# A one-core hybrid attention and state-space block: denser attention pieces, inputs loaded three ahead, and six split tiles

## The chip, the cores and the metric

The kernel runs on one core of one Trainium2 chip. The metric is device time in microseconds (us), the median of several runs; a profiled execution gives the trace.

## The reference

One layer of a residual block on 256 tokens of width 4096. All products are in float32 accuracy.

```python
h = rms_norm(x, pre_norm_gain)
proj = h @ w_in                                   # one projection, columns split into:
(q, k, v, gate_a, qi, ki, wi, z, xs, bm, cm, dt_raw, merge_logits) = split(proj)
q, k, qi, ki = (apply_rope(a) for a in (q, k, qi, ki))
attn = dsa_attention(q, k, v, qi, ki, wi * scale) # indexer: top 64 keys of each query, then softmax
y_a  = attn * silu(gate_a)
y_b  = ssd_mixer(xs, z, bm, cm, dt_raw, ...)      # Mamba-2 scan, gated and normed
gates = sigmoid(merge_logits)                     # one gate of width 4096 for each branch
merged = gates[0] * (y_a @ w_branch_attn) + gates[1] * (y_b @ w_branch_ssd)
x + rms_norm(merged @ w_out, post_norm_gain)
```

## The kernel before

**The matmuls.** Each float32 matrix is held as a high and a low part, and a product is three matmuls (low x high, high x low, high x high) of 128x512 on the matrix engine (PE). The inputs are split once; the weights are split as they stream in: a `raw` tile of 512 KB is loaded on the SP queue, ACT rounds it into `wh`, DVE subtracts for `wl`. There are four `wh` and four `wl` buffers of two rows of weights each (`SBUFS`). `gemm` does 512 output columns in this way (`w_qi`, the first q and k columns, the last two of `w_out`).

**Pairs.** `pair_gemm` does 1024 output columns over 256 inner rows a step. A step of kind S is a Strassen-like form with 7 products (21 matmuls of PE) and needs an `ext` tile of input combinations; kinds D and R have 8 products (24 matmuls). An S step costs DVE more, since it also combines weights. The tuples `SX`, `SY`, `SM`, `SG` say which of the 16 steps are of kind S in which stage; those named `plain` are done as R there. A POOL-issued DMA adds one weight row to another for each S step.

**The order of the stages:** `w_qi` and the small columns with the indexer's scores and top-k; q and k of the first group; then for four groups of heads `w_qk[j]` and `w_vg[j]`; `w_z` and `w_x` with the state-space work; eight `w_gate` pairs; eight branch pairs (`w_br`, for two groups of output columns n the attention branch and then the SSD branch); three `w_out2` pairs and the two `w_out` columns.

**Pieces.** Everything that is not a weight matmul (rotation, attention, scan, the combination of inputs) is a Python generator of small pieces in the queue `aux`. A stage calls `step(pace)` once a step of kind S and twice a step of kind D or R; `pace` pieces are emitted at each call, with a carried fraction. The attention of group j (`attend`: 18 pieces, each a few instructions, and a last one that writes `yraw` to DRAM scratch `yscr`) is queued when `w_vg[j]` ends, so it runs in the next pair, `w_qk[j+1]` or, for the last group, `w_z[0]`. The list scheduler of the framework then settles each engine's order, which is fixed from there on.

**The end of a pair.** `early` is emitted behind the last S step: it drains what is left of the pieces, takes the four output tiles (`outs`) and starts to combine the PSUM banks into them, with one ACT copy and two DVE additions (lines 545 to 547). In `w_qk` and `w_z[0]` these output tiles are `yr0` to `yr3`; `attend` uses `yr0` for its result, `yr1` and `yr2` as `yraw`, and `yr3`.

**Inputs of the later stages.** `forms_from` turns 256 rows of branch input (from `yscr`, during the last `w_gate` pair and the first branch pair) or of merged input (from `mscr`, during the last branch pairs and `w_out2[0]`) into a split base tile and, for S steps, an `ext` tile. It loads one 256 KB tile `fr` ahead of the one that it works on, by a DMA on the POOL queue, into two buffers. `ev_branch` makes the merged input: sigmoid times product, summed over the two branches, transposed into `mT`, and written to `mscr` in one DMA for each 512 columns.

Of the kernel before, what the change touches and what calls it, by code (L numbers as in the profile page):

```python
# [17 lines left out]
P = 128  # L18
# [29 lines left out]
def fused_block(tc, x, xT, w_qi, w_misc, w_q0, w_qk, w_vg, w_x, w_z, w_gate, w_br, w_out2, w_out,  # L48
# [98 lines left out]
    def load_half(raw, chunk, hf, each=False):  # L147
# [3 lines left out]
        else:  # L151
            nc.sync.dma_start(raw, chunk[:, hf * HK:(hf + 1) * HK, :])

    def gemm(chunks, nk, act, evac, prep=None, plan=None, done=None, pace=1):
        while len(live) > 1:
            drain(live.popleft())
# [5 lines left out]
        for n, (half, toks) in enumerate(plan):  # L162
            c, hf = divmod(half, KC // HK)
            if half not in raws:
                raws[half] = raw_tile()
                if prep is not None:
                    if not hf:
                        xr = prep_x(c)
                    load_half(raws[half], chunks[c], hf, c == 0)
                else:  # L170
                    load_half(raws[half], chunks[c], hf)
            if half not in parts:
                wh = whp.tile([P, HK, NW], F32R, tag="wh", name="wh")
                wl = wlp.tile([P, HK, NW], F32R, tag="wl", name="wl")
                parts[half] = wh, wl
                if len(parts) > SBUFS:
                    del parts[next(iter(parts))]
                rs = raws[half]
                if prep is not None:
                    for i in range(HK):  # L180
                        split_x(half * HK + i, xr[:, hf * HK + i, :])
                        A.activation(wh[:, i, :], rs[:, i, :], AF.Copy)  # L182
                        V.tensor_sub(wl[:, i, :], rs[:, i, :], wh[:, i, :].bitcast(F32))
                else:
                    A.activation(wh, rs, AF.Copy)  # L185
# [57 lines left out]
    mb = [attp.tile([P, (t + 1) * P], F32, name=f"mb{t}") for t in range(2)]  # L243
    qip_cm, qip = open_pool("qip", bufs=2)
    startp, sp = open_pool("startp", bufs=2)

    def prep_x(c):
        xr = sp.tile([P, KC, S], F32, tag="xr", name="xr")
# [399 lines left out]
        turn(mode)  # L648

    def forms_from(what, load, seven, pairs, diff=True):  # L650
        a = load(pairs[0])
        for i in pairs:
            ahead = load(i + 1) if i + 1 in pairs else None
            make_base(i, a)
            yield
            make_ext(i, a, seven, diff)
            kind_of[i] = what
            a = ahead
            yield

    def kinds(seven, pairs, plain=()):
# [156 lines left out]
    for j in range(4):  # L818
        if j:
            pair_gemm("x", "aux", lambda i: w_qk[j - 1, i], kinds(SX, range(16)), yr4_after(0),  # L820
                      ev_qk(j))
        pair_gemm("x", "aux", lambda i: w_vg[j, i], kinds(SX, range(16)), yr4_after(4), ev_vg(j), pace=0.4)


# [175 lines left out]
    def z_pair(m, seven, outs, hooks={}, pace=1.25):  # L1000
# [2 lines left out]

    more = [i for i in SX if i not in SS]
    z_pair(0, SX, yr4_after(0), {more[-1] + 1: lambda: push(remake(
        more, SS, lambda: attp.tile([P, 2, S], F32, tag="lm", bufs=2, name="fr")))}, 1)
    drain()
    attp_cm.__exit__(None, None, None)
    ssdp_cm, ssdp = open_pool("ssdp")
# [15 lines left out]
        return run  # L1025

    def load_y(i):
        a = tp.tile([P, 2, S], F32, tag="fr", bufs=2, name="fr")
        nc.gpsimd.dma_start(a.rearrange("p k t -> p (k t)"), yscr[i])
        return a  # L1030

    def load_m(i):
        a = tp.tile([P, 2, S], F32, tag="fr", bufs=2, name="fr")
# [6 lines left out]
    def grow():  # L1040
        for n, i in enumerate(grown):
            ext_tag[i] = f"eg{n}"
        return remake(grown, SG, lambda: tp.tile([P, 2, S], F32, tag="fr", bufs=2, name="fr"))

    for g, cols in enumerate(GATES):
        last = g == len(GATES) - 1
# [44 lines left out]
    def ev_branch(n, br):  # L1091
        def run(c):
# [12 lines left out]
                for _ in range(4):  # L1105
                    yield
            for b in range(2):
                if (n, b) == (6, 1):
                    m2 = [brp.tile([P, 2, S], F32, tag=f"sg{h}", name="mT") for h in range(2)]
                    for t in range(2):  # L1110
                        transpose4(c[2 * t + b], m2[0][:, :, t * P:(t + 1) * P], A,
                                   m2[1][:, :, t * P:(t + 1) * P])
                        yield
                    merged.update({14 + h: m2[h] for h in range(2)})
                    continue
                mT = brp.tile([P, 4, S], F32, tag="mT", name="mT")
                for t in range(2):
                    transpose4(c[2 * t + b], mT[:, :, t * P:(t + 1) * P], A)
                    yield
                if n < 6:  # L1120
                    nc.scalar.dma_start(mscr[n + b], mT.rearrange("p k t -> p (k t)"))
                else:
                    for h in range(2):
                        merged[2 * (n + b) + h] = mT[:, 2 * h:2 * h + 2, :]
            yield
        return run

# [22 lines left out]

    def open_og():
        ogp["cm"], p = open_pool("ogp")
        ogp["og"] = [[p.tile([P, 2, NW], F32, name=f"og{t}_{n}") for n in range(3)]
                     for t in range(2)]
        ogp["oss"] = p.tile([P, 2, 8], F32, name="oss")
        V.memset(ogp["oss"], 0.0)

    def ogs(n):
        def run():
            og = ogp["og"]  # L1160
            return [og[t][n // 2][:, b, :] for t in range(2) for b in range(2)]
# [17 lines left out]

    for n in range(0, 6, 2):  # L1180
        if n == 0:
            order = (0, 2, 5, 1, 3, 8, 4, 9, 6, 11, 7, 10, 12, 13, 14, 15)
            plain = (9, 10, 14)
        else:
            order, plain = range(16), ()
        plan = [(i, "R" if k == "D" else k) for i, k in kinds(SM, order, plain)]
# [178 lines left out]
```

## Time and profile before

| | us |
|---|---|
| median of 3 runs (2848.03 to 2849.34) | 2849.27 |
| the profiled execution, its own time | 2850.78 |
| its span, first to last instruction | 2849.0 |
| PE busy | 2795.8 (98%) |
| DVE busy | 2514.9 (88%) |
| ACT busy | 1801.8 (63%) |
| mean granted TensorE clock | 0.994 |

A busy share is a mean over stages; the time of a stage is read against what its matmuls take in a stage that holds nothing else. The matmuls overlap on PE, so the length of one in a row is longer than the distance from one to the next.

### The profile page before, as it was taken

The page shows a single profiled execution, that of the slowest core. Times are in us where ns is not written, and L with a number is a line of the kernel's source. Part 1 is how long each engine was busy: PE and PEld are TensorE (multiplying, and loading weights), DVE is VectorE, ACT ScalarE, POOL GpSimd, SP SyncE. Part 2 cuts the span into 40 slices and gives each one's busy share as a digit, 9 for nine tenths or more (in the row PEclk, how much of TensorE's full clock was granted, in tenths as well). Part 3 has the DMA queues.
Part 4 walks back from the last instruction along what each step waited for, and adds up shares of the span by engine and source line. Part 5 has one row for each costly group of instructions (what it writes and reads, how often), then busy time and mean ns, then how long its engine had stood idle before and what let it go on. Part 6 is the DMA issues. An engine that isn't in the chain of part 4 may idle for free.

```text
span 2849.0 us, 36823 instructions
## 1 busy us (share of the span) xinstructions
PE 2795.8 (98%) x12597; PEld 2287.5 (80%) x12597; DVE 2514.9 (88%) x3326; ACT 1801.8 (63%) x2533; POOL 222.1 (8%) x265
## 2 busy tenths in 40 slices
PE   9999999999999999999999999999999999999998
PEld 7877787787877878787888788888877888878886
DVE  6668998998989979898898999999977999988975
ACT  7444565665656756878788866666655655655653
POOL 0100000000000000000000010110100000000000
PEclk9999999999999999999999999999999999999999
DMA  9545776776767767666767788888877888877874
GB/s 366 187 162 167 212 228 203 237 219 198 233 199 239 219 199 222 187 209 207 230 183 216 221 256 252 255 250 258 269 232 243 253 266 271 263 221 234 266 260 140
DMA packets 205756, 650.41 MB, mean 228 GB/s; under 512 B 23168, under 2 KB 23936, under 8 KB 205568
## 3 DMA queue, kind: packets, MB, share of 16 engines
q1 hardware_dynamic: 163728, 567.05, 59.3%
q0 software_dynamic: 34064, 65.29, 13.2%
q10 hardware_dynamic: 7776, 15.73, 1.4%
q8 instruction: 98, 1.61, 0.2%
q14 instruction: 90, 0.74, 0.1%
HBM read 628.06 MB, written 19.92 MB: 227 GB/s over the span
## 4 chain that ended last, share of the span: by engine, by line
PE 79%; DVE 10%; issue 6%; DMA 3%; ACT 2%; POOL 0%; SPq 0%; DVEq 0%; ACTq 0%; POOLq 0%
PE p L541 66%; PE p L194 3%; PE p L196 3%; PE p L195 3%; DVE wl L498 2%; DVE raw L610 1%; DMA yscr<-yraw 1%; DVE wl L186 1%; DMA fr<-yscr 1%; DVE raw L609 1%; ACT wh L494 1%; DVE wl L612 1%; DMA fr<-mscr 1%; DVE wl L605 1%; PE p L364 0%
## 5 line engine op out<-in xcount | busy, mean ns | idle before, releaser
L541 PE MATMUL p<-wh,b 128*128 128x512 f32 x4330 | 1428.7, 394 | 1.0 <-ACT wh L494 0.5
L494 ACT ACTIVATE wh<-raw 128x1024 fp32r<-128x1024 f32 (+1 forms) x1117 | 1052.8, 970 | 592.5 <-DVE raw L609 280.1
L498 DVE TENSOR_TENSOR wl<-raw,wh 128x1024 fp32r<-128x1024 f32 (+1 forms) x890 | 953.7, 1088 | 60.4 <-ACT wh L494 53.7
L541 PEld LDWEIGHTS p<-wh,b 128*128 128x128 f32 x4330 | 815.9, 188 | 173.8 <-ACT wh L494 5.0
L541 PE MATMUL p<-wl,b 128*128 128x512 f32 x2165 | 848.0, 392 | 10.3 <-DVE wl L496 8.0
L541 PE MATMUL p<-wh,ext 128*128 128x512 f32 x2396 | 806.9, 392 | 14.1 <-DVE pc L546 12.8
L541 PEld LDWEIGHTS p<-wh,ext 128*128 128x128 f32 x2396 | 451.2, 188 | 110.9 <-DVE pc L546 15.4
L541 PEld LDWEIGHTS p<-wl,b 128*128 128x128 f32 x2165 | 408.4, 189 | 96.4 <-DVE wl L496 10.4
L541 PE MATMUL p<-wl,ext 128*128 128x512 f32 x1198 | 473.8, 395 | 8.3 <-DVE wl L612 7.5
L496 DVE SCALAR_TENSOR_TENSOR wl<-raw,wh 128x1024 fp32r<-128x1024 f32 x227 | 276.9, 1220 | 39.2 <-ACT wh L494 38.1
L541 PEld LDWEIGHTS p<-wl,ext 128*128 128x128 f32 x1198 | 225.5, 188 | 68.2 <-DVE wl L612 16.3
L610 DVE TENSOR_TENSOR raw<-raw 128x1024 f32<-128x1024 f32 x221 | 270.3, 1223 | 5.6
L186 DVE TENSOR_TENSOR wl<-raw,wh 128x1024 fp32r<-128x1024 f32 x112 | 138.8, 1239 | 90.3 <-ACT wh L185 90.1
L604 ACT ACTIVATE wh<-raw 128x512 fp32r<-128x512 f32 x221 | 138.8, 628 | 105.4 <-PE p L541 97.7
L185 ACT ACTIVATE wh<-raw 128x1024 fp32r<-128x1024 f32 x112 | 118.3, 1058 | 136.3 <-PE p L196 124.5
L194 PE MATMUL p<-wh,b 128*128 128x512 f32 x512 | 202.1, 396 | 2.0 <-ACT wh L182 2.0
L195 PE MATMUL p<-wl,b 128*128 128x512 f32 x512 | 200.0, 391 | 0.0
L196 PE MATMUL p<-wh,b 128*128 128x512 f32 x512 | 199.8, 390 | 0.0
L605 DVE TENSOR_TENSOR wl<-raw,wh 128x512 fp32r<-128x512 f32 x221 | 151.5, 685 | 16.8 <-ACT wh L604 15.7
L609 DVE TENSOR_TENSOR raw<-raw 128x512 f32<-128x512 f32 x221 | 152.2, 689 | 5.0
L612 DVE TENSOR_TENSOR wl<-raw,wh 128x512 fp32r<-128x512 f32 x221 | 151.1, 684 | 0.0
L606 ACT ACTIVATE wh<-raw 128x512 fp32r<-128x512 f32 x221 | 136.3, 617 | 0.0
(243 smaller groups left out, 1841.4 us busy)
## 6 DMA issues: line engine op xcount, KB each, us to landing
raw<-w_gate_d SPq DMA_DIRECT2D x256, 512.0 KB, 5.7
raw<-w_vg_d SPq DMA_DIRECT2D x128, 512.0 KB, 5.5
raw<-w_x_d SPq DMA_DIRECT2D x128, 512.0 KB, 5.1
raw<-w_br_d SPq DMA_DIRECT2D x128, 512.0 KB, 5.5
raw<-w_out_d SPq DMA_DIRECT2D x128, 512.0 KB, 5.2
raw<-w_qk_d SPq DMA_DIRECT2D x96, 512.0 KB, 5.6
raw<-w_z_d SPq DMA_DIRECT2D x64, 512.0 KB, 5.5
raw<-w_qi_d SPq DMA_DIRECT2D x62, 512.0 KB, 5.2
```

The costliest lines, as they stand in the source:

```text
L186: V.tensor_sub(wl, rs, wh.bitcast(F32))
L194: T.matmul(ps[t], al[:, tk], wh[:, i, :], start=first, stop=False)
L195: T.matmul(ps[t], ah[:, tk], wl[:, i, :], start=False, stop=False)
L196: T.matmul(ps[t], ah[:, tk], wh[:, i, :], start=False, stop=last)
L494: A.activation(h, src, AF.Copy, scale=float(sign))
L496: V.scalar_tensor_tensor(l, src, -1.0, fbit(h), ALU.mult, ALU.subtract)
L498: V.tensor_sub(l, src, fbit(h))
L541: T.matmul(ps[j], l, r, start=first and n == 0, stop=left[j] == 0 and n == 2)
L605: V.tensor_sub(l[:, 1, :], ra[:, 1, :], fbit(h[:, 1, :]))
L609: V.tensor_sub(ra[:, 1, :], ra[:, 0, :], ra[:, 1, :])
L610: V.tensor_sub(rb, rb, ra[:, 1:2, :].to_broadcast([P, 2, NW]))
L612: V.tensor_sub(l[:, 0, :], ra[:, 0, :], fbit(h[:, 0, :])))
```

## The change

- The pieces in `w_qk[j]` (three pairs) and in `w_z[0]` are emitted at pace 1.25 instead of 1.
- `forms_from` loads three tiles ahead, and the tag `fr` has four buffers instead of two.
- `mT` becomes two tiles of 256 KB in `yr0` to `yr3` for each 512 columns, so ACT copies each transposed block in two halves, and `mscr` is written in two DMAs. For the last two groups of columns these tiles are used where they lie.
- `w_out2[0]` takes its steps in another order, and steps 4 and 7 become R there.
- The output tiles `og` lie otherwise: one of six pairs moves to `yr4` and `yr5`, and that of the last columns to an `ext` buffer.
- A pool `morep` gives `gemm` two more `wh` and `wl` buffers until the end of the first q columns; of every six halves, four use the old buffers and two the new.

```diff
+XBUFS = 2
+    slots = {"more": None, "n": 0}
+
+    def next_split():
+        hp, lp = whp, wlp
+        if slots["more"] is not None:
+            slots["n"] += 1
+            if slots["n"] % (SBUFS + XBUFS) >= SBUFS:
+                hp, lp = slots["more"]
+        return (hp.tile([P, HK, NW], F32R, tag="wh", name="wh"),
+                lp.tile([P, HK, NW], F32R, tag="wl", name="wl"))
...
-                wh = whp.tile([P, HK, NW], F32R, tag="wh", name="wh")
-                wl = wlp.tile([P, HK, NW], F32R, tag="wl", name="wl")
+                wh, wl = next_split()
...
     def forms_from(what, load, seven, pairs, diff=True):
-        a = load(pairs[0])
-        for i in pairs:
-            ahead = load(i + 1) if i + 1 in pairs else None
+        coming = deque(load(i) for i in pairs[:3])
+        for n, i in enumerate(pairs):
+            if n + 3 < len(pairs):
+                coming.append(load(pairs[n + 3]))
+            a = coming.popleft()
             make_base(i, a)
             yield
             make_ext(i, a, seven, diff)
...
             pair_gemm("x", "aux", lambda i: w_qk[j - 1, i], kinds(SX, range(16)), yr4_after(0),
-                      ev_qk(j))
+                      ev_qk(j), pace=1.25)
...
     z_pair(0, SX, yr4_after(0), {more[-1] + 1: lambda: push(remake(
-        more, SS, lambda: attp.tile([P, 2, S], F32, tag="lm", bufs=2, name="fr")))}, 1)
+        more, SS, lambda: attp.tile([P, 2, S], F32, tag="lm", bufs=2, name="fr")))})
...
-        a = tp.tile([P, 2, S], F32, tag="fr", bufs=2, name="fr")
+        a = tp.tile([P, 2, S], F32, tag="fr", bufs=4, name="fr")
         nc.gpsimd.dma_start(a.rearrange("p k t -> p (k t)"), yscr[i])
...
-                mT = brp.tile([P, 4, S], F32, tag="mT", name="mT")
+                m2 = [yr.tile([P, 2, S], F32, tag=f"yr{2 * b + h}", name="mT") for h in range(2)]
                 for t in range(2):
-                    transpose4(c[2 * t + b], mT[:, :, t * P:(t + 1) * P], A)
+                    transpose4(c[2 * t + b], m2[0][:, :, t * P:(t + 1) * P], A,
+                               m2[1][:, :, t * P:(t + 1) * P])
                     yield
-                if n < 6:
-                    nc.scalar.dma_start(mscr[n + b], mT.rearrange("p k t -> p (k t)"))
+                for h in range(2):
+                    if n < 6:
+                        nc.scalar.dma_start(mscr[n + b][:, 2 * h * S:2 * (h + 1) * S],
+                                            m2[h].rearrange("p k t -> p (k t)"))
+                    else:
+                        merged[2 * (n + b) + h] = m2[h]
...
-            order = (0, 2, 5, 1, 3, 8, 4, 9, 6, 11, 7, 10, 12, 13, 14, 15)
-            plain = (9, 10, 14)
+            order = (0, 2, 4, 5, 7, 1, 9, 3, 8, 6, 11, 10, 12, 13, 14, 15)
+            plain = (4, 7, 9, 10, 14)
```

What the change does to the order on an engine is shown at two places. Lines of the changed kernel are 11 to 14 higher there (494 is 507, 545 is 558, 604 and 606 are 617 and 619, 762 is 776, 790 is 804).

ACT near the end of the pair `w_qk[0]`, before: `pT` is the last transposed softmax block of the attention, `yraw` its result, and L545 the copy with which `early` begins; `wh` are weight splits.

```order
L762 ACTIVATE pT<-p_4204 128x512
L494 ACTIVATE wh<-raw 128x1024 x3
L367 ACTIVATE yraw<-p_4266 128x2x128
L368 ACTIVATE yraw<-p_4266 128x2x128
L790 DMA yscr<-yraw 128x512 x2
L545 ACTIVATE pc<-p_3587 128x512
```

The same place in the changed kernel:

```order
L776 ACTIVATE pT<-p_4114 128x512
L507 ACTIVATE wh<-raw 128x1024 x3
L617 ACTIVATE wh<-raw 128x512
L380 ACTIVATE yraw<-p_4185 128x2x128
L381 ACTIVATE yraw<-p_4185 128x2x128
L804 DMA yscr<-yraw 128x512 x2
L619 ACTIVATE wh<-raw 128x512
L507 ACTIVATE wh<-raw 128x512
L507 ACTIVATE wh<-raw 128x1024 x3
L558 ACTIVATE pc<-p_3591 128x512
```

The write to `yscr` stood directly ahead of the copy of `early`, and five splits of weights now stand between them. On PE, counted from the start of this pair, the last transposes of the attention stood behind 337 weight matmuls and now stand behind 288; the value products of its last unit stood 21 weight matmuls behind the transposes that they need, and now stand 5 behind.

The POOL queue from the last `w_gate` pairs to the end, before (`raw` rows are the additions for S steps):

```order
L588 DMA raw<-w_gate_d 128x512 x13
L1029 DMA fr<-yscr 128x512
L588 DMA raw<-w_gate_d 128x512 x2
L1029 DMA fr<-yscr 128x512
L588 DMA raw<-w_gate_d 128x512 x51
L1029 DMA fr<-yscr 128x512 x14
L588 DMA raw<-w_br_d 128x512 x8
L1034 DMA fr<-mscr 128x512 x2
L588 DMA raw<-w_br_d 128x512 x16
L1034 DMA fr<-mscr 128x512 x9
L588 DMA raw<-w_out_d 128x512
L1034 DMA fr<-mscr 128x512
```

The same in the changed kernel:

```order
L601 DMA raw<-w_gate_d 128x512 x13
L1045 DMA fr<-yscr 128x512 x3
L601 DMA raw<-w_gate_d 128x512 x2
L1045 DMA fr<-yscr 128x512
L601 DMA raw<-w_gate_d 128x512 x51
L1045 DMA fr<-yscr 128x512 x12
L601 DMA raw<-w_br_d 128x512 x8
L1050 DMA fr<-mscr 128x512 x2
L601 DMA raw<-w_br_d 128x512
L1050 DMA fr<-mscr 128x512 x2
L601 DMA raw<-w_br_d 128x512 x15
L1050 DMA fr<-mscr 128x512 x8
```

Four branch inputs instead of two, and four merged inputs instead of two, are asked for ahead of the run of loads, and no load of a merged input stands behind an addition for `w_out` any more.

## Rows read from the trace of the kernel before

**Rows 1.** The page: busy us, share of the span and instructions of three engines (PEld is the load of the stationary operand, beside PE).

```profile
PE 2795.8 (98%) x12597; PEld 2287.5 (80%) x12597; DVE 2514.9 (88%) x3326; ACT 1801.8 (63%) x2533; POOL 222.1 (8%) x265
```

**Rows 2.** Busy time by stage: start and end in us, length, then busy us and (xcount) of PE, PEld, DVE, ACT, POOL, the granted TensorE clock, DMA share and GB/s. In order: the second q/k column, `w_vg[0]`, `w_qk[0]`, `w_vg[1]`, `w_vg[2]`, `w_vg[3]`, `w_x[0]`, the third gate pair, the last gate pair, the first branch pair (n=0), the attention branch of n=2 and of n=6, and `w_out2[0]`. A window counts one to three instructions of its neighbours too.

```profile
259.25:304.46 45.21, 44.66 (x201) 36.76 (x200) 44.67 (x84) 24.46 (x33) 1.88 (x2) 1.00 0.62 191
304.46:388.75 84.29, 83.10 (x367) 67.49 (x366) 81.26 (x100) 52.91 (x68) 7.77 (x9) 1.00 0.80 233
388.75:477.62 88.87, 88.87 (x419) 73.94 (x417) 77.53 (x98) 58.87 (x89) 7.79 (x9) 1.00 0.73 216
477.62:567.98 90.36, 86.06 (x375) 69.00 (x373) 85.09 (x106) 50.96 (x66) 7.07 (x9) 0.98 0.72 215
656.86:746.28 89.42, 85.57 (x374) 67.56 (x373) 85.27 (x106) 51.07 (x66) 7.58 (x9) 1.00 0.73 215
835.22:925.77 90.55, 85.80 (x374) 69.00 (x373) 85.34 (x106) 51.18 (x66) 7.80 (x9) 0.98 0.72 215
1014.70:1103.40 88.70, 84.97 (x365) 69.89 (x363) 72.73 (x80) 51.75 (x63) 6.08 (x7) 0.96 0.70 212
1655.48:1736.40 80.92, 80.92 (x359) 67.03 (x357) 75.53 (x85) 52.23 (x65) 8.46 (x10) 1.00 0.84 259
2059.06:2149.26 90.20, 87.14 (x376) 69.75 (x374) 71.79 (x109) 50.75 (x69) 7.67 (x13) 1.00 0.73 242
2149.26:2197.19 47.93, 44.87 (x194) 35.91 (x193) 34.09 (x45) 25.88 (x32) 3.37 (x5) 1.00 0.77 245
2237.99:2281.18 43.19, 43.03 (x197) 35.14 (x196) 41.73 (x52) 25.88 (x33) 4.58 (x6) 1.00 0.85 261
2406.02:2449.66 43.64, 43.45 (x197) 34.97 (x196) 43.22 (x58) 28.23 (x39) 4.24 (x6) 1.00 0.84 269
2493.18:2586.11 92.93, 87.92 (x384) 72.21 (x382) 76.75 (x96) 50.79 (x66) 6.10 (x8) 0.96 0.75 226
```

**Rows 3.** The view of waits: engine and line that waited, for whom, us in total, times, longest.

```profile
POOL fr L1029 <- DVE ext L465: 53.5, 9, 11.4
DVE pc L546 <- DMA yscr<-yraw: 31.4, 4, 8.5
ACT b L471 <- DMA fr<-yscr: 31.1, 13, 4.3
ACT b L471 <- DMA fr<-mscr: 16.1, 7, 5.4
```

**Rows 4.** The timeline round the end of `w_qk[0]`: start, length, engine, line, operation, and in brackets the idle time before it and what ended it.

```profile
473.55 0.38 ACT L368 ACTIVATE yraw<-p 128x256 f32<-128x256 f32 x1
473.68 0.84 ACTq L790 DMA_DIRECT2D yscr<-yraw  x2
474.56 0.60 ACT L545 ACTIVATE pc<-p 128x512 f32<-128x512 f32 x1 [0.64 <-ACT yraw L368]
475.10 1.06 ACT L494 ACTIVATE wh<-raw 128x1024 fp32r<-128x1024 f32 x1
...
481.69 0.69 DVE L546 TENSOR_TENSOR pc<-p,pc 128x512 f32<-128x512 f32 x1 [8.05 <-DMA yscr<-yraw]
...
482.44 0.79 PE L541 MATMUL p<-wh,ext 128*128 128x512 f32 x1 [3.30 <-DVE pc L546]
```

**Rows 5.** Busy time (columns as in rows 2) in the 3 us ahead of that matmul, in the stretches behind the stalls at 482 and at 1019 us, and behind one at 2504 us.

```profile
479.00:482.00 3.00, 0.14 (x1) 0.00 (x0) 0.30 (x1) 0.00 (x0) 0.00 (x0) 1.00 1.05 295
482.44:484.00 1.56, 1.56 (x4) 1.27 (x5) 1.56 (x2) 0.00 (x0) 0.00 (x0) 0.50 0.03 4
...
1019.90:1025.00 5.10, 5.04 (x12) 4.03 (x13) 5.10 (x9) 1.06 (x2) 0.00 (x0) 0.50 0.00 0
...
2504.00:2510.00 6.00, 5.98 (x14) 4.73 (x15) 3.97 (x4) 0.83 (x1) 0.00 (x0) 0.51 0.88 247
```

**Rows 6.** The timeline in the last gate pair: the load of one branch input on POOL, and the ACT instruction that takes it.

```profile
2101.36 0.54 POOL L1029 DMA_DIRECT2D fr<-yscr  x1 [7.64 <-DVE ext L465]
...
2107.35 0.63 ACT L471 ACTIVATE b<-fr 128x512 fp32r<-128x512 f32 x1 [2.29 <-DMA fr<-yscr]
```

**Rows 7.** The timeline round the start of `w_out2[0]` (L471 takes a merged input; L563 begins to gather the last branch pair, L1094 multiplies it by its gates, L496 splits the weights of the second step).

```profile
2497.98 0.63 ACT L471 ACTIVATE b<-fr 128x512 fp32r<-128x512 f32 x1 [5.36 <-DMA fr<-mscr]
2498.51 0.58 ACT L563 ACTIVATE pc<-p 128x512 f32<-128x512 f32 x1
...
2494.03 1.29 DVE L1094 TENSOR_TENSOR pc<-pc,sg 128x512 f32<-128x512 f32 x2
2499.13 0.69 DVE L1094 TENSOR_TENSOR pc<-pc,sg 128x512 f32<-128x512 f32 x1 [3.81 <-ACT pc L563]
...
2502.74 1.22 DVE L496 SCALAR_TENSOR_TENSOR wl<-raw,wh 128x1024 fp32r<-128x1024 f32 x1
...
2504.02 0.80 PE L541 MATMUL p<-wl,b 128*128 128x512 f32 x1 [5.01 <-DVE wl L496]
```

**Rows 8.** DMA issues: name, queue, xcount, KB each, median us from issue to landing; and from the timeline at the end of the attention branch of n=6, the last write of merged input, the DVE additions of `early` and of the instructions behind it.

```profile
mscr<-mT ACTq DMA_DIRECT2D x6, 512.0 KB, 3.7
...
yscr<-yraw ACTq DMA_DIRECT2D x8, 256.0 KB, 8.1
...
2437.53 0.33 ACTq L1121 DMA_DIRECT2D mscr<-mT  x1
...
2446.37 0.68 DVE L547 TENSOR_TENSOR pc<-p,pc 128x512 f32<-128x512 f32 x1
```

More of the change, by code (lines that the diff above doesn't have):

```diff
@@ L245, in fused_block @@
     startp, sp = open_pool("startp", bufs=2)
+    more_cm, morep = open_pool("morep", bufs=XBUFS)
+    slots["more"] = morep, morep
     def prep_x(c):
@@ L657, in forms_from @@
             kind_of[i] = what
-            a = ahead
             yield
@@ L803, in fused_block @@
     drain(top)
+    slots["more"] = None
+    more_cm.__exit__(None, None, None)
     startp.__exit__(None, None, None)
@@ L1032, in load_m @@
     def load_m(i):
-        a = tp.tile([P, 2, S], F32, tag="fr", bufs=2, name="fr")
+        a = tp.tile([P, 2, S], F32, tag="fr", bufs=4, name="fr")
         nc.gpsimd.dma_start(a.rearrange("p k t -> p (k t)"),
@@ L1042, in grow @@
             ext_tag[i] = f"eg{n}"
-        return remake(grown, SG, lambda: tp.tile([P, 2, S], F32, tag="fr", bufs=2, name="fr"))
+        return remake(grown, SG, lambda: tp.tile([P, 2, S], F32, tag="fr", bufs=4, name="fr"))
     for g, cols in enumerate(GATES):
@@ L1107, in run @@
             for b in range(2):
[L1108 to L1115, printed above, removed]
-                mT = brp.tile([P, 4, S], F32, tag="mT", name="mT")
+                m2 = [yr.tile([P, 2, S], F32, tag=f"yr{2 * b + h}", name="mT") for h in range(2)]
                 for t in range(2):
-                    transpose4(c[2 * t + b], mT[:, :, t * P:(t + 1) * P], A)
+                    transpose4(c[2 * t + b], m2[0][:, :, t * P:(t + 1) * P], A,
+                               m2[1][:, :, t * P:(t + 1) * P])
                     yield
-                if n < 6:
-                    nc.scalar.dma_start(mscr[n + b], mT.rearrange("p k t -> p (k t)"))
-                else:
-                    for h in range(2):
-                        merged[2 * (n + b) + h] = mT[:, 2 * h:2 * h + 2, :]
+                for h in range(2):
[4 more added lines that the diff above has]
+                        merged[2 * (n + b) + h] = m2[h]
             yield
@@ L1152, in open_og @@
         ogp["cm"], p = open_pool("ogp")
-        ogp["og"] = [[p.tile([P, 2, NW], F32, name=f"og{t}_{n}") for n in range(3)]
-                     for t in range(2)]
+        for t, n in ((0, 0), (1, 0), (0, 2), (1, 2), (0, 4)):
+            o = p.tile([P, 2, NW], F32, name=f"og{t}_{n}")
+            ogp.update({(t, n + b): o[:, b, :] for b in range(2)})
         ogp["oss"] = p.tile([P, 2, 8], F32, name="oss")
@@ L1159, in run @@
         def run():
-            og = ogp["og"]
-            return [og[t][n // 2][:, b, :] for t in range(2) for b in range(2)]
+            if n == 4:
+                ogp.update({(1, n + b): yr.tile([P, NW], F32, tag=f"yr{4 + b}", name="og1")
+                            for b in range(2)})
+            return [ogp[t, n + b] for t in range(2) for b in range(2)]
         return run
@@ L1200, in og @@
     def og(t, n):
-        if n < 6:
-            return ogp["og"][t][n // 2][:, n % 2, :]
-        return o6[:, t, :] if n == 6 else yr.tile([P, NW], F32, tag=f"yr{4 + t}", name="o7")
+        return ogp[t, n] if n < 6 else o67[n - 6][:, t, :]
     fin_cm, fin = open_pool("fin")
-    o6 = extb.tile([P, 2, NW], F32, tag=f"eb{SX[7]}", name="o6")
+    o67 = [extb.tile([P, 2, NW], F32, tag=f"eb{SX[7 + n]}", name="o67") for n in range(2)]
     res, pgs = {}, {}
@@ L1226, in load_x @@
             for t in range(2):
-                res[t, i] = r[:, t, :] if i < 7 else tp.tile([P, NW], F32, tag="fr", bufs=2, name="xr")
+                res[t, i] = r[:, t, :] if i < 7 else tp.tile([P, NW], F32, tag="fr", bufs=4, name="xr")
                 nc.sync.dma_start(res[t, i], x[t * P:(t + 1) * P, i * NW:(i + 1) * NW])
```

## Prediction

> **What bounds the kernel now.** The page comes first: PE is busy for 98% of the span and the load of its stationary operand for 80% [rows 1]. That is a mean over forty stages, and it hides the answer, so I cut the span into stages and read busy time stage by stage [rows 2]. The third gate pair holds nothing but 357 weight matmuls, and takes 80.92 us: 0.22667 us for each. This is the clean rate. The attention branch of n=2 has 180 of them and 16 transposes: 43.19 - 180 x 0.22667 = 2.39 us for 16 transposes, 0.15 each. With these two prices a stage has a clean time, and what it takes beyond is waiting, or a slower clock. So PE bounds the kernel, and a change can only win the excess of a stage, or lose by adding to it or to the matmuls.
>
> The excesses [rows 2]: `w_vg[1]` has 357 matmuls and 16 transposes, 83.31 clean, and takes 90.36: 7.05. `w_vg[2]` 6.11, `w_vg[3]` 7.24, `w_x[0]` (363 matmuls, 82.28) 6.42. `w_vg[0]`, with 8 transposes, 2.17. The last gate pair (375, 85.00) 5.20, the first branch pair (192, 43.52) 4.41, `w_out2[0]` (366 and 16 transposes, 85.35) 7.58. The second q/k column (192 and 8) 0.49. The view of waits says who is waited for [rows 3], and the timelines show the places.
>
> **Step A: the denser pieces.** At the end of `w_qk[0]`, ACT issues the write of `yraw` at 473.68 and DVE's second instruction of `early` starts at 481.69, after 8.05 us of waiting for that write: the output tile is the buffer that the write still reads [rows 4]. Such waits come four times, 31.4 us in all [rows 3], once for each attention. PE has PSUM banks to go on with for a while, so that it idles only 3.30 us, up to 482.44. Behind the stall the granted clock is 0.50, the lower of the two levels (1.2 GHz): in the 1.56 us from 482.44 four matmuls are counted, where the clean rate gives seven; the same after `w_z[0]`, 5.10 us at 0.50 with 12 matmuls where 22 fit [rows 5]. Stall and slow stretch together are the excess of the stage that follows. In `w_vg[2]` the mean clock is 1.00, so there was the stall alone.
>
> The change moves the last transposes from 337 to 288 weight matmuls into the pair: 49 x 0.22667 = 11.1 us earlier. The write would be issued near 473.68 - 11.1 = 462.6 and land, with the median 8.1 us of such writes [rows 8], near 470.7. The first copy of `early` ends at 474.56 + 0.60 = 475.16 [rows 4], and DVE needs the tile then. The margin is some 4.5 us, so the wait goes.
>
> What it can win lies between two bounds. All four excesses: 7.05 + 6.11 + 7.24 + 6.42 = 26.8. The nearest stage without such a wait is `w_vg[0]`, which still has 2.17; if three stages keep as much, 26.8 - 6.5 = 20.3. What it costs: the value products of the last unit stand 5 matmuls (1.13 us) behind their transposes, instead of 21. ACT's copy between takes about 0.6 (the copy of the same shape at 474.56), and a split of 1.06 us may stand ahead of it [rows 4]; 0.58 + 1.06 - 1.13 = 0.5, for four pairs 2. DVE has 77.53 us of work in the 88.87 of `w_qk[0]` [rows 2]; the same work comes earlier, and 11.3 us of DVE are free to take it. Should waits on DVE come back in the pairs, half is left: 12. I take 24 less the cost and a small rest, **21**, nearer to `w_vg[0]`, the one stage of this form that shows what is left without the wait.
>
> **Step B: three loads ahead.** In the last gate pair a load of `fr` was held on POOL for 7.64 us, until DVE had finished with the buffer, and issued at 2101.36; ACT stood idle for 2.29 us until it landed, at 2107.35 [rows 6]. Thirteen such waits of ACT sum to 31.1, and POOL waits 53.5 for the buffers [rows 3]. Behind ACT's waiting instruction stand the splits of weights, for which PE waits. With three loads ahead, a buffer is asked for two conversions earlier, and the load has some 12 us and more, against the 6 us from 2101.36 to 2107.35. The bound is the excess of the two stages, 5.20 + 4.41 = 9.6; the lower one is 3, if DVE's work on the ext tiles holds PE instead (it has 71.79 of 90.20 there, so it isn't full) [rows 2]. I take **8**.
>
> **Step C: the order of `w_out2[0]`.** Its excess is one stall of 5.01 us at 2504.02, and the slow stretch behind it, 14 matmuls in 6.00 us at a clock of 0.51 [rows 5, 7]. The chain runs backwards so: PE waits for a weight split of DVE, DVE for ACT's copy, and ACT stood for 5.36 us at the conversion of a merged input until 2497.98. With more loads ahead and the inputs needed in another order, that wait goes; the gathering of the last branch pair stays. From 2499.13 to 2502.74 DVE took 3.61 us for it, and the split 1.22. Starting where DVE's work before had ended, 2494.03 + 1.29 = 2495.32, this gives 2500.15. PE has by then done a first step of 24 matmuls, to 2493.18 + 5.44 = 2498.62: a stall of 1.5 is left, and stalls of that size leave the clock alone, as `w_vg[2]` shows for a longer one. Steps 4 and 7 as R add 6 matmuls, 1.36. So 7.58 - 1.5 - 1.36 = 4.7. One more base and ext fall into the attention branch of n=6, where DVE is full, 43.22 of 43.64 [rows 2]: 1 us for it. I take **3.7**; the bounds are 7.58 - 1.36 = 6.2 and, if another wait takes its place and the 6 matmuls come on top, -1.
>
> **Step D: two more split tiles.** In `w_qi` and the first q column PE is held by nothing of this kind; only what comes behind can gain, when top-k and the ext tiles are done earlier: 0.49 + 2.17 = 2.7 at most, in the second q/k column and `w_vg[0]` [rows 2]. Below, 0. I take **1**.
>
> **Step E: the merged blocks in `yr0` to `yr3`.** ACT's extra halves cost it some 0.2 us a block, and it has 28.23 us of work in 43.64 [rows 2]. The buffers are the same as the output tiles of the next attention branch. In before, the last write of merged input is issued at 2437.53 and the tile would be needed by the DVE addition at 2446.37: 8.84 us later, and 512 KB to `mscr` landed in 3.7 [rows 8]. So **0**, with a bound of three stages, at some 6 us each (the price of such a wait in step A), 18.
>
> The sum: 21 + 8 + 3.7 + 1 = 33.7. From the profiled execution's 2850.78 this is 2817.1. That execution lies 1.5 above the median of the runs, so the forecast is **2816**. Its own range is 2806 to 2826: step A at its bound of 26.8 and C at 6.2 on one side, A at 15 and B at 4 on the other. All the bounds at once would be 26.8 + 9.6 + 6.2 + 2.7 = 45.3, 2804.
>
> **The rivals.**
>
> (a) The gains come in part, since other waits stand behind those that go: A 12, B 4, C 1, D 0, 17 in all, **2832**. For it: DVE has 85 of 90 us of work in the `w_vg` stages [rows 2], so that a queue which starts late can't catch up. Against it: `w_vg[0]` has 81.26 in 84.29 and little excess.
>
> (b) Writes of merged input hold up the output tiles of the following branch pair, as `yraw` does now. It decides from 8.84 us between issue and landing. For it: the writes of 256 KB to `yscr` needed 8.1, with the DMA engines saturated (share 1.05 at 479 to 482) [rows 5, 8]. Against it: the writes to `mscr`, in the very stages concerned, 3.7. 33.7 - 18 = 15.7, **2834**.
>
> The Trainium skill, in "DMA: Bandwidth & Descriptors", section "Anatomy of one DMA — SWDGE (gpsimd) path", fits a DMA of that path as 2.0 us and its bytes at 436 GB/s: for 256 KB an estimate of 2.6 us, by which (b) would have no chance. These writes go by ACT's queue and not that path, and the row of 8.1 us is three times as long, so the measurement decides, and (b) keeps a chance.
>
> (c) The attention's write still lands after `early` wants the tile, so that step A doesn't do what it says: the pieces come earlier in the order, but DVE, with 77.53 of 88.87 us of work, executes them late. The margin of 4.5 us would have to go. 12.7 are left, **2837**.
>
> (d) (b) and (c) together: 33.7 - 21 - 18 = -5, 2854.6, within 0.2% of before.
>
> (e) The other side: in the denser pairs each piece stands nearer to the one it needs, so PE waits for the softmax chain between them. If every one of the 72 attention pieces (18 in four pairs) cost one step of that distance, 5 matmuls or 1.13 us, this would be 81 us, and **2897**. It decides from (33.7 + 5.7) / 1.13 = 35 pieces on. For it: PE runs without a gap in `w_qk[0]` now, 88.87 of 88.87, so nothing shows how much slack there is [rows 2]. Against it: the pace grows by only a quarter, and with 9 S and 7 D steps there are 9 + 14 = 23 calls, 28.75 pieces at this pace, so that some 357 / 28.75 = 12 matmuls are left between two pieces.
>
> **Chances.** 0.55 for the forecast, 0.20 for (a), 0.06 for (b), 0.06 for (c), 0.07 for (d), 0.06 for (e). A difference under 0.2% (5.7 us) is what a measurement of this kernel can't tell from none. The range from 2806 to 2838 takes in the forecast, (a), (b) and (c), nearly 0.87 less the tails. Faster 0.87, same 0.07, slower 0.06.
>
> **What would show it.** A: no row in which DVE waits for the `yscr` write at L546's successor, and the excess of the three `w_vg` stages and of `w_x[0]` down from 6 or 7 to about 2, with a clock of 1.00; the pairs `w_qk` still without gaps on PE. B: ACT's waits for `fr` gone, the last gate pair near 85 to 86, the first branch pair near 44. C: `w_out2[0]` near 89.2, with one short stall. D: the second q/k column near 44.7. E: no wait of the output tiles for `mscr`. The forecast is wrong if PE now idles inside the `w_qk` pairs, if the stages behind them keep an excess over 4 each, or if the branch stages grow.

## The result, and the profile after

The changed kernel takes 2809.97 us (median of 4 runs, 2809.73 to 2811.88), the kernel before beside it 2848.65: a ratio of 0.9866, with a 95% interval from 0.9849 to 0.9883. It is faster by 38.7 us, where 33 were forecast; the time lies in the range. The profiled execution has a span of 2808.0 us instead of 2849.0.

The page of the changed kernel (columns as in [rows 1]), and its stages (as in [rows 2]), in order `w_vg[0]`, `w_qk[0]`, `w_vg[1]`, `w_vg[2]`, `w_vg[3]`, `w_x[0]`, the last gate pair, the first branch pair, the attention branch of n=6, `w_out2[0]`, and the second q/k column:

```profile
PE 2782.5 (99%) x12603; PEld 2282.5 (81%) x12603; DVE 2508.4 (89%) x3316; ACT 1803.2 (64%) x2541; POOL 220.4 (8%) x263
```

```profile
306.31:388.20 81.89, 81.89 (x367) 67.81 (x365) 78.38 (x92) 52.08 (x66) 7.78 (x9) 1.00 0.80 237
388.20:477.17 88.97, 88.97 (x418) 73.82 (x417) 81.31 (x105) 58.73 (x89) 7.78 (x9) 1.00 0.73 218
477.17:560.78 83.61, 83.60 (x374) 68.04 (x373) 81.74 (x102) 52.03 (x66) 7.77 (x9) 1.00 0.79 235
649.76:733.33 83.57, 83.56 (x374) 68.02 (x373) 81.73 (x102) 52.06 (x66) 7.81 (x9) 1.00 0.79 231
822.32:905.91 83.59, 83.58 (x374) 68.04 (x373) 81.73 (x102) 52.04 (x66) 7.80 (x9) 1.00 0.78 233
994.88:1077.16 82.28, 82.28 (x364) 68.15 (x363) 69.16 (x75) 49.94 (x60) 6.08 (x7) 1.00 0.73 226
2032.86:2118.10 85.24, 85.24 (x376) 70.32 (x375) 75.64 (x117) 52.80 (x74) 8.19 (x14) 1.00 0.79 259
2118.10:2161.62 43.52, 43.52 (x193) 36.04 (x192) 29.21 (x36) 23.17 (x27) 2.18 (x3) 1.00 0.79 254
2370.45:2415.37 44.92, 44.48 (x198) 34.65 (x196) 44.68 (x63) 30.57 (x46) 4.60 (x7) 1.00 0.84 265
2458.89:2545.06 86.17, 86.17 (x389) 71.48 (x388) 68.03 (x81) 47.21 (x60) 5.36 (x7) 1.00 0.71 225
260.02:306.31 46.29, 44.67 (x201) 36.75 (x200) 45.43 (x86) 25.71 (x35) 1.88 (x2) 1.00 0.62 189
```

PE is now busy in nearly all of almost every row, at a clock of 1.00. Against [rows 2], the three `w_vg` stages are shorter by 6.75, 5.9 and 7.0 us and `w_x[0]` by 6.4, while the four denser pairs grew by 0.3 together: 25.7 us from step A. The last gate pair and the first branch pair gave 5.0 and 4.4, 9.4 from step B. `w_out2[0]` gave 6.8, and the attention branch of n=6 cost 1.3: 5.5 from step C. The rest of the 41.0 is 0.5 at the start, to which the section on step D comes.

In the view of waits no row is left in which DVE waits for the write to `yscr`. Lines are 13 higher here: L484 is the conversion that was L471, L478 was L465, L554 was L541, L559 and L560 were L546 and L547, and L625 was L612.

```profile
POOL fr L1045 <- DVE ext L478: 34.2, 6, 8.6
ACT b L484 <- DMA fr<-yscr: 11.4, 5, 4.1
ACT b L484 <- DMA fr<-mscr: 5.1, 4, 2.6
```

The timeline round the end of `w_qk[0]`, which answers to [rows 4], ACT's rows and then DVE's, and below it the median landing of the writes (columns as in [rows 8]):

```profile
462.19 0.82 ACTq L804 DMA_DIRECT2D yscr<-yraw  x2
...
469.50 0.58 ACT L558 ACTIVATE pc<-p 128x512 f32<-128x512 f32 x1
...
470.77 0.68 DVE L559 TENSOR_TENSOR pc<-p,pc 128x512 f32<-128x512 f32 x1
...
mscr<-mT ACTq DMA_DIRECT2D x12, 256.0 KB, 3.5
...
yscr<-yraw ACTq DMA_DIRECT2D x8, 256.0 KB, 4.2
```

The write is issued at 462.19 (462.6 was forecast). It lands, at the median, in 4.2 us instead of 8.1, so near 466.4, and DVE takes the tile at 470.77, without waiting. ACT's first copy of `early` comes at 469.50, 5 us earlier than before: it had stood behind the late write on ACT.

### The profile page after: what moved, and what is told of

Same layout as the page of the kernel before. It is cut to its first block, busy times and chain, and to the rows that moved or that the text cites. A ratio compares the mean times of both kernels' runs of the same rounds, so it can differ in the third digit from the quotient of the medians.

```text
span 2808.0 us, 36830 instructions
## 1 busy us (share of the span) xinstructions
PE 2782.5 (99%) x12603; PEld 2282.5 (81%) x12603; DVE 2508.4 (89%) x3316; ACT 1803.2 (64%) x2541; POOL 220.4 (8%) x263
## 3 DMA queue, kind: packets, MB, share of 16 engines
q8 instruction: 99, 1.62, 0.2%
## 4 chain that ended last, share of the span: by engine, by line
PE 93%; DVE 4%; ACT 1%; issue 1%; DMA 0%; SPq 0%; DVEq 0%; ACTq 0%
PE p L554 77%; PE p L205 4%; PE p L206 4%; PE p L207 4%; PE p L377 1%; DVE wl L511 1%; ACT wh L507 1%; DVE raw L623 0%; PE p L408 0%; PE p L921 0%; PE p L786 0%; PE p L753 0%; DVE cacc L857 0%; DVE raw L622 0%; DVE og L1255 0%
## 5 line engine op out<-in xcount | busy, mean ns | idle before, releaser
L554 PE MATMUL p<-wh,b 128*128 128x512 f32 x4350 | 1431.8, 393 | 0.6 <-ACT wh L507 0.5
L554 PEld LDWEIGHTS p<-wh,b 128*128 128x128 f32 x4350 | 816.6, 188 | 170.6 <-ACT wh L507 3.6
L554 PE MATMUL p<-wl,b 128*128 128x512 f32 x2175 | 848.8, 390 | 0.0
L554 PE MATMUL p<-wh,ext 128*128 128x512 f32 x2380 | 796.8, 390 | 1.5 <-ACT wh L507 1.0
L554 PEld LDWEIGHTS p<-wh,ext 128*128 128x128 f32 x2380 | 446.9, 188 | 94.2 <-ACT wh L507 2.9
L554 PEld LDWEIGHTS p<-wl,b 128*128 128x128 f32 x2175 | 408.8, 188 | 82.6 <-DVE wl L509 0.4
L554 PE MATMUL p<-wl,ext 128*128 128x512 f32 x1190 | 469.1, 394 | 3.6 <-DVE wl L625 3.4
L554 PEld LDWEIGHTS p<-wl,ext 128*128 128x128 f32 x1190 | 223.4, 188 | 63.3 <-DVE wl L625 11.1
L625 DVE TENSOR_TENSOR wl<-raw,wh 128x512 fp32r<-128x512 f32 x219 | 149.7, 684 | 0.0
```

The lines of the kernel that those rows point to most:

```text
L554: T.matmul(ps[j], l, r, start=first and n == 0, stop=left[j] == 0 and n == 2)
L625: V.tensor_sub(l[:, 0, :], ra[:, 0, :], fbit(h[:, 0, :])))
```

## The experiments

**1. The pace alone.**

```diff
 # the kernel before
-                      ev_qk(j))
+                      ev_qk(j), pace=1.25)
-        more, SS, lambda: attp.tile(...)))}, 1)
+        more, SS, lambda: attp.tile(...)))})
```

> The kernel before with pace 1.25 in the three w_qk pairs and in w_z[0], nothing else. My theory (the write of yraw lands before early wants the tile): DVE's waits for yscr<-yraw gone, the stages w_vg[1..3] and w_x[0] fall by 6.8, 5.9, 7.0 and 6.4 us as in the changed kernel, so 25 to 26 us in all, near 2823 us. Rival (a part of this comes from another edit, such as the buffers of the merged blocks or the split tiles): 12 to 20 us, 2829 to 2837.

Measured: 2822.81 us beside 2845.96 of before, a ratio of 0.9911 (0.9894 to 0.9928). The stages `w_vg[1]` and `w_x[0]` of its trace, as in [rows 2]:

```profile
476.68:560.28 83.60, 83.59 (x375) 68.05 (x373) 81.67 (x102) 52.02 (x66) 7.89 (x10) 1.00 0.78 236
994.44:1076.72 82.28, 82.28 (x365) 68.13 (x364) 69.15 (x75) 49.94 (x60) 6.08 (x7) 1.00 0.75 230
```

They are those of the changed kernel to 0.01 us, and `w_vg[2]` (83.62) and `w_vg[3]` (83.59) to 0.05, so step A needs no other edit. The medians differ by 23.2 us, a little less than the 25 to 26 expected; the kernel before beside it took 2844.27 to 2855.55.

**2. No write behind the output tiles, at the old pace.** The rotated q of the group is written in place of the attention's result, and at the start of the attention; the result `yraw` is left out of the output.

```diff
 # the kernel before
+        for i in range(2):
+            nc.scalar.dma_start(yscr[2 * j + i], qT[:, 2 * i:2 * i + 2, :]...)
         units = [(t, h0) for t in range(2) for h0 in (0, 2)]
...
-        for i in range(2):
-            nc.scalar.dma_start(yscr[2 * j + i], yraw[i]...)
```

> The kernel before at its pace 1. The DMA to yscr reads the rotated q of the group instead of yraw and is issued at the start of the attention, so that no write reads yr1 and yr2 when early takes them; yraw is still computed but goes nowhere, and the attention branch gets other data. Nothing is emitted denser. My theory (the tile that the write still reads is the whole cause): as much is won as by the denser pieces, 24 to 27 us, near 2823 us. Rival (it is the crowding of late pieces on ACT and DVE at the end of the pair that holds early and the next pair, the wait for the DMA only lying on top): at most half, 2836 us or more.

Measured: 2824.52 us, 0.9914 (0.9896 to 0.9933). By the medians this is 21.4 us, under the 24 to 27 expected, but far from the rival's half. `w_vg[1]` takes 83.44, `w_vg[2]` 83.96, `w_vg[3]` 83.59 and `w_x[0]` 82.28, together 25.8 us less than in [rows 2], with no piece emitted denser:

```profile
387.81:476.76 88.95, 88.95 (x419) 73.95 (x418) 80.60 (x103) 58.90 (x89) 8.51 (x10) 1.00 0.75 218
476.76:560.20 83.44, 83.44 (x375) 68.07 (x374) 82.55 (x103) 51.45 (x66) 7.04 (x9) 1.00 0.77 233
```

This shows the cause apart from the crowding of pieces, which is as before here: the tile that a write still reads.

**3. Two doses in one kernel.** The changed kernel with `pace=1.07` in the four pairs.

> The changed kernel with pace 1.07 in those four pairs. The last transposes stand 333 weight matmuls into w_qk[0] and w_qk[1] (4 earlier than at pace 1), 312 into w_qk[2] and 316 into w_z[0] (25 and 21 earlier). My theory (PE has 8.05 - 3.30 = 4.8 us of other work while DVE waits, so that a write which lands 4.8 to 5.7 us earlier costs PE nothing): w_vg[1] and w_vg[2] keep a stall of 1 to 3 us, w_vg[3] and w_x[0] are as fast as at 1.25 (83.6 and 82.3). In all 9 to 13 us over the changed kernel. Rival (the gain goes in proportion to how much earlier the write lands): w_vg[3] and w_x[0] keep half of their excess, 3 us each, in all some 17 us over the changed kernel.

Measured: 2824.05 us, 0.9915 (0.9895 to 0.9935). By stages it is 14.5 us over the changed kernel: `w_vg[1]` 89.46, `w_vg[2]` 89.26, `w_vg[3]` 84.85, `w_x[0]` 83.97.

```profile
477.49:566.95 89.46, 85.57 (x374) 67.65 (x373) 85.57 (x107) 51.31 (x66) 7.80 (x9) 1.00 0.75 218
834.00:918.85 84.85, 83.97 (x375) 68.15 (x374) 83.67 (x104) 51.20 (x66) 7.82 (x9) 1.00 0.78 232
```

The waits behind it, DVE's first and PE's then, in `w_vg[1]`, and busy time in the 48 us that follow the wait (columns as in [rows 2]):

```profile
479.89 0.69 DVE L559 TENSOR_TENSOR pc<-p,pc 128x512 f32<-128x512 f32 x1 [5.79 <-DMA yscr<-yraw]
...
480.63 0.50 PE L554 MATMUL p<-wh,ext 128*128 128x512 f32 x1 [1.63 <-DVE pc L559]
...
482.76 0.51 PE L554 MATMUL p<-wh,b 128*128 128x512 f32 x1 [0.47 <-DVE pc L560]
...
489.02 0.50 PE L554 MATMUL p<-wl,ext 128*128 128x512 f32 x1 [0.54 <-DVE wl L625]
...
482.00:530.00 48.00, 45.74 (x199) 35.39 (x198) 47.97 (x65) 25.73 (x35) 3.47 (x4) 1.00 0.64 182
```

Neither side had it right. PE's first stall is 1.63 us, half of the 3.30 of [rows 4], and the clock stays at 1.00. Yet the stage loses 5.9 us, nearly as much as before. PE is stopped again, at 489.02 and later (at 506.50 and 523.04, 0.60 and 0.19 us), by DVE's weight splits. Its idle time in the stage is 3.89 us in all, and its busy time is 1.97 longer than in the changed kernel, of which no row says the reason. What counts is DVE. It has 85.57 us of work in this stage, and PE's clean time is 83.31; waiting 5.79 us, it falls behind and stays behind: in the 48 us that follow, it is busy for 47.97. In the changed kernel it is as busy there (47.94 in the same 48 us), but it enters them without the delay, and PE doesn't stop. In the changed kernel DVE does 81.31 us in `w_qk[0]` and 81.74 in `w_vg[1]`; before, 77.53 and 85.09 [rows 2]. The sum is the same within 0.5, and 3.8 us of it had been pushed by the wait from a stage with room into one without. In `w_vg[2]` DVE waits 5.96 us and 5.7 are lost. For `w_vg[3]` the write is issued 9.1 us ahead of the stage's start, instead of 4.0 in the kernel before; DVE waits 1.46, and 1.3 are lost; in `w_x[0]`, where DVE has 72.93 of 83.97, 3.32 us of waiting cost 1.7.

**4. The other side: denser still.** The changed kernel with `pace=2` in the four pairs.

> The changed kernel with pace 2 in those four pairs. The last transposes stand 193 weight matmuls into w_qk[0] instead of 288, and value products stand 4 matmuls (0.9 us) behind the transposes that they need. My theory: the write has landed long before anyway, nothing is left to win, and PE waits at some products for ACT's copy, 0.5 us each at most, so 0 to 6 us over the changed kernel. The rival of the prediction (each piece that follows the one it needs by 5 matmuls or fewer costs PE about 1.1 us): 4 pairs with 8 such pieces, 35 us over the changed kernel.

Measured: 2811.01 us, 0.9869 (0.9852 to 0.9886).

```profile
388.84:477.68 88.84, 88.84 (x419) 73.76 (x418) 81.37 (x104) 59.04 (x89) 7.80 (x9) 1.00 0.73 217
477.68:561.18 83.50, 83.50 (x374) 67.95 (x373) 81.77 (x102) 51.92 (x66) 7.80 (x9) 1.00 0.80 236
```

PE has no gap in `w_qk[0]` even with products 4 matmuls behind their transposes. Of the four pairs only `w_z[0]` is longer than in the changed kernel, by 0.5 us (89.47). Rival (e) has next to no price here, and from pace 1.25 on nothing is left to win.

**5. Two buffers again, and one load ahead.** In the changed kernel; the first edit is the same at all four places where the tag `fr` stands, of which one is shown:

```diff
 # two_buffers
-        a = tp.tile([P, 2, S], F32, tag="fr", bufs=4, name="fr")
+        a = tp.tile([P, 2, S], F32, tag="fr", bufs=2, name="fr")
```

```diff
 # one_ahead
-        coming = deque(load(i) for i in pairs[:3])
+        coming = deque(load(i) for i in pairs[:1])
-            if n + 3 < len(pairs):
-                coming.append(load(pairs[n + 3]))
+            if n + 1 < len(pairs):
+                coming.append(load(pairs[n + 1]))
```

> The changed kernel with two fr buffers again, still asking for three tiles ahead. My theory (what held the loads was the release of the buffer, not the place where they are asked for): POOL waits for the buffers as before, and the last gate pair and the first branch pair go back from 85.25 and 43.52 to about 90 and 48 us, w_out2[0] too loses a few us: 9 to 14 us over the changed kernel, near 2820 to 2824 us. Rival (asking earlier in the program is what helps): within 2 us of the changed kernel.

> The changed kernel, with forms_from asking for one tile ahead instead of three, and four buffers. The order of the instructions on all five engines and queues comes out the same as in the changed kernel, one for one. My theory (the buffers alone, since the scheduler lifts a load to the place where its buffer allows it): the same time as the changed kernel, 2810 us, every stage within 0.3 us. Rival (the depth matters, by waits that the order does not show): 5 to 9 us more in the last gate pair and the first branch pair.

Measured: with two buffers 2826.73 us, 0.9922 (0.9907 to 0.9937); with one load ahead and four buffers 2811.22, 0.9868 (0.9853 to 0.9883), the changed kernel's time and 15.5 us less. With one load ahead the last gate pair takes 85.00, the first branch pair 43.52 and `w_out2[0]` 86.12, and its trace has the instructions of every engine in the changed kernel's order, one for one. The waits with two buffers, and its last gate pair, first branch pair, attention branch of n=6 and `w_out2[0]`:

```profile
POOL fr L1045 <- DVE ext L478: 56.9, 10, 11.1
ACT b L484 <- DMA fr<-yscr: 31.6, 14, 4.0
...
ACT b L484 <- DMA fr<-mscr: 17.4, 8, 4.4
```

```profile
2032.90:2123.70 90.80, 88.03 (x377) 71.22 (x375) 73.06 (x110) 52.07 (x70) 7.69 (x13) 0.98 0.72 241
2123.70:2170.62 46.92, 44.74 (x193) 35.74 (x192) 33.00 (x44) 24.75 (x31) 3.38 (x5) 1.00 0.79 248
2379.47:2425.62 46.15, 44.22 (x197) 34.81 (x196) 43.32 (x58) 28.93 (x43) 4.26 (x6) 1.00 0.82 252
2469.14:2561.80 92.66, 89.01 (x390) 73.32 (x389) 70.64 (x85) 48.01 (x62) 6.03 (x7) 0.96 0.69 219
```

ACT's waits are back near the 31.1 and 16.1 of [rows 3], and the four stages together lose 16.7 us; that is above the 9 to 14 expected, since `w_out2[0]` loses 6.5 of them. So the buffers are the whole of step B, and "three ahead" is a name without effect: the list scheduler places a load where its buffer lets it, whatever the depth. `w_out2[0]`, with the new order of steps, falls back to 92.66, which was 92.93 with the old one: PE stalls there for 3.65 us, behind a conversion on ACT that waited 4.44 for its load.

**6. Three buffers.** The same line with `bufs=3`.

> The changed kernel with three fr buffers. My theory (a load needs the time in which two tiles are worked on, and a third buffer gives most of it): the last gate pair and the first branch pair within 2 us of 85.0 and 43.5, w_out2[0] within 1 us of 86.2, in all 0 to 4 us over the changed kernel. Rival (the fourth buffer is needed): 90 and 47 us in those two stages as with two buffers, 9 us over.

Measured: 2812.74 us, 0.9871 (0.9854 to 0.9889). The last gate pair takes 87.31, the first branch pair 43.52 and `w_out2[0]` 86.11; ACT's waits for `fr` from `yscr` are 14.3 us. A third buffer gives all but the 2 us of the last gate pair.

**7. The old order of steps in `w_out2[0]`**, in the changed kernel:

```diff
-            order = (0, 2, 4, 5, 7, 1, 9, 3, 8, 6, 11, 10, 12, 13, 14, 15)
-            plain = (4, 7, 9, 10, 14)
+            order = (0, 2, 5, 1, 3, 8, 4, 9, 6, 11, 7, 10, 12, 13, 14, 15)
+            plain = (9, 10, 14)
```

> The changed kernel with the order of steps of before in w_out2[0], with steps 4 and 7 of kind S again: 6 matmuls (1.36 us) fewer. My theory of the prediction (the conversion held by its load made the stall at the start of this pair, and the loads alone take it away): w_out2[0] at 85.3 to 87 us against 86.17, the attention branch of n=6 at 43.7 against 44.92, so 0 to 3 us under the changed kernel. Rival (DVE has not the time for the ext tiles of early S steps while it gathers the last branch pair, and two early R steps are what helps): a stall of 3 to 5 us and a slow stretch come back, w_out2[0] at 90 us or more, 3 to 7 us over the changed kernel.

Measured: 2809.30 us, 0.9861 (0.9844 to 0.9877), beside 2811.22 of the kernel with one load ahead on the same chip, too little to tell by the times. The attention branch of n=6 and `w_out2[0]`:

```profile
2371.42:2416.35 44.93, 44.50 (x198) 34.66 (x196) 44.69 (x63) 30.62 (x46) 4.80 (x7) 1.00 0.84 264
2459.87:2544.73 84.86, 84.86 (x384) 70.28 (x382) 73.78 (x91) 50.17 (x66) 6.24 (x8) 1.00 0.77 237
```

`w_out2[0]` is 1.31 us shorter than with the new order, which is the price of 6 matmuls (1.36), and PE has no gap either way. The new order buys nothing; the buffers took the stall away. The attention branch of n=6, expected back at 43.7, stays at 44.93: with the old order too DVE does one more base and `ext` there, 63 instructions instead of the 58 of [rows 2], and is full. With two buffers they are 58 again (experiment 5), so the two more buffers bring them, and not the order.

**8. Four split tiles**, in the changed kernel:

```diff
-    more_cm, morep = open_pool("morep", bufs=XBUFS)
-    slots["more"] = morep, morep
...
-    slots["more"] = None
-    more_cm.__exit__(None, None, None)
```

> The changed kernel without the two more split tiles. By the stages of the profiles (+1.1 us in the four w_qi and first q stages, +1.1 in the second q/k column, -2.4 in w_vg[0], -0.3 at the start): these stages go back to the times of before, w_vg[0] to 84.3 and the second q/k column to 45.2, and the kernel is 0.5 us slower, not to be told from no change. Rival (w_vg[0] was won by another edit): w_vg[0] stays at 81.9 and the kernel is 2 us faster than the changed one.

Measured: 2809.44 us, 0.9862 (0.9848 to 0.9877). The second q/k column and `w_vg[0]`:

```profile
257.82:303.02 45.20, 44.65 (x201) 36.75 (x200) 44.66 (x84) 24.51 (x33) 1.88 (x2) 1.00 0.60 194
303.02:387.36 84.34, 83.07 (x367) 67.50 (x365) 81.28 (x100) 52.98 (x68) 7.79 (x9) 1.00 0.78 232
```

The split tiles do win 2.4 us in `w_vg[0]`, since DVE's work moves ahead (81.28 against 78.38 there). They lose 1.1 in the second q/k column, where DVE is now full (45.43 of 46.29) and PE waits 1.62 us at one place, and 1.4 in the four stages between the first `w_qi` stage and that column (207.38 with six tiles, 205.98 with four). These times repeat within 0.1 us in every run with the same number of tiles, so they aren't chance; why the four stages take longer stays open. The sum is 0.0.

**9. More S steps, to beat both.** Order and kinds as in experiment 7, with `plain = ()` there and S steps in the first branch pair; beside it the changed kernel once more.

> The changed kernel with the order of steps of before in w_out2[0], and with no step done as R for want of an ext tile there (9, 10 and 14 are S) nor in the first branch pair (1, 3, 4 and 6 are S). 8 + ... : 6 matmuls fewer by the order, 9 by the three steps and 12 by the four, 27 x 0.22667 = 6.1 us. In the trace of the changed kernel the ext tiles are ready (all of the branch input by 2129, 11 us into the first branch pair) and DVE has 29.2 us of work in 43.5 there and 68.0 in 86.2. My theory (with the loads early, PE's matmuls alone bound these stages): the first branch pair at 40.8, w_out2[0] at 82.8, near 2804 us. Rival (the weight combinations that S steps ask of DVE bring the waits back at the start of w_out2[0], where DVE gathers the last branch pair): w_out2[0] at 86 us or more, near 2808 us.

> The changed kernel as it is, beside the other two on the same chip: 2810 us, the last gate pair 85.0 to 85.3, the first branch pair 43.52, w_out2[0] 86.1 to 86.2 by every theory.

Measured: 2809.02 us, 0.9862 (0.9844 to 0.9879), and the changed kernel 2811.11, 0.9867 (0.9852 to 0.9883). The first branch pair and `w_out2[0]`, and a row of the view of waits:

```profile
2117.60:2161.40 43.80, 42.07 (x182) 33.48 (x181) 43.72 (x59) 29.11 (x39) 3.44 (x4) 1.00 0.80 237
2458.00:2543.00 85.00, 84.14 (x374) 67.87 (x373) 81.95 (x105) 54.17 (x77) 8.64 (x10) 1.00 0.79 230
...
PEld p L554 <- DVE wl L625: 15.5, 27, 1.4
```

With 12 matmuls fewer the first branch pair isn't shorter: DVE's work goes from 29.21 to 43.72, and fills the 43.80. `w_out2[0]` has 9 matmuls fewer than in experiment 7, and takes 85.00 where it took 84.86. Neither side had the number for it (82.8, or 86 and more). The rival had the engine right, but not the place: PE's stops are at 2505.90 and 2526.48, far behind the start of the stage. An S step trades PE's time for DVE's. No version here beats the changed kernel by what can be told apart; the old order of experiment 7 is the better choice by its stage.

## Why the prediction was right, and where its terms were off

**Step A, right in its mechanism, 21 forecast and 25.7 found.** The rest of 2.17 us that I carried over from `w_vg[0]` doesn't belong to such a stage: it was that stage's own, and gone in it too (81.89), by step D. The 2 us for pieces close behind each other were 0.3. The working held two errors that cancelled. The landing was taken at 8.1 us after the issue, and it is 4.2 in the changed kernel; the need was taken at 475.16, and it is at 470.77, since ACT's copy had itself been late behind the write. The margin came out at 4 us as forecast, by chance. And "stall and slow stretch together are the excess" doesn't carry over: experiment 3 lost 5.9 us in a stage whose clock stayed at 1.00, through DVE's backlog. The kernel before shows it too: I read `w_vg[2]`, with a clock of 1.00 and an excess of 6.11, as the stall alone, and its stall is 2.17 us:

```profile
660.54 0.50 PE L541 MATMUL p<-wh,ext 128*128 128x512 f32 x1 [2.17 <-DVE pc L546]
```

So what rival (a) gave as its reason, that DVE can't catch up in the `w_vg` stages, was right; what it lacked is that the queue no longer starts late. That PE has work to go on with for 4.8 us, on which I counted in experiment 3, is no cover where DVE is full.

**Step B, 8 forecast and 9.4 found**, and for the reason that the rows gave: POOL held for the buffer. Experiment 5 shows that asking earlier has no share in it.

**Step C, 3.7 forecast and 5.5 found.** The stall went altogether; the 1.5 us that I left of it didn't come. The cost in the attention branch of n=6 was 1.3, for 1, by one more base and `ext` as forecast; but the two more buffers bring them there, not the order. The credit was misplaced: the gain is the buffers' alone, and the order costs 1.3 in `w_out2[0]` (experiments 5 and 7).

**Step D, 1 forecast, 0 found** (experiment 8). The mechanism was only half of it: 2.4 us are won in `w_vg[0]`, and 2.5 are lost in five stages, a cost for which the sum had no term. The 0.5 us at the start are chance: two executions of the changed kernel differ by 1.1 us in the first `w_qi` stage (44.89 and 45.98).

**Step E, 0 forecast, 0 found.** No wait of an output tile for `mscr`; the writes land in 3.5 us, and the branch stages behind them take their clean time (43.21 for n=2, 43.19 before). No run takes this edit, or the other places of `og`, out alone, so a small price of theirs isn't excluded. Rivals (b) and (d) fall with it, and (c) with experiment 1; (a) had the waits of DVE come back, and DVE in the `w_vg` stages fell from 85.1 to 81.7 us instead.

The sum was 33.7 against 41.0 of the two spans; 4.7 of the difference are in step A. The lower end of the forecast's own range, 2806, doesn't come out of its two bounds, which give 2807.7.

## What to carry to other kernels

Where a helper engine is nearly full in a stage, a wait that it suffers just ahead can cost the main engine almost its whole length, even if the main engine's first stall is short (5.8 us of waiting cost 5.9 here; with room in the stage, 3.3 cost 1.7): compare its work in the stage with the stage's clean time. Ask of a late load whether its buffer or its place in the program holds it, since with a scheduler only the buffer may count. A form with fewer matmuls pays only as long as the engine that prepares it has room.

## What the runs showed of the hardware that was not expected

Writes of 256 KB from the same queue landed in 8.1 us at the median where they were issued at the end of a pair, and in 4.2 where they were issued 11 us earlier. Earlier isn't faster by itself: at pace 2 they were issued another 22 us earlier in `w_qk[0]`, and the median was 5.9; at pace 1.07 it was 6.4. In the 8 us behind the late write the DMA engines were 0.93 busy, in the 4 us behind the early one 0.91, so the mean share doesn't tell the two apart, and why they differ stays open. The rows, before and then after:

```profile
473.70:481.70 8.00, 5.44 (x24) 4.16 (x23) 0.01 (x1) 2.97 (x5) 1.15 (x2) 1.00 0.93 261
```

```profile
462.20:466.40 4.20, 4.20 (x20) 3.48 (x19) 4.13 (x6) 2.45 (x4) 0.86 (x1) 1.00 0.91 273
```
